# Latent layer: order of its first sums, place of the rotary work, transposes, and a last projection by token

## The chip, the cores and the metric

The kernel runs on one core of one Trainium2 chip. A core has five engines with queues of their own: TensorE (PE; PEld is its loading of weights), VectorE (DVE), ScalarE (ACT), GpSimd (POOL) and SyncE (SP), which issues most transfers. The metric is the device time of one execution in microseconds (us).

## The reference

Two blocks over 256 tokens of width 2048 in float32 stand one behind the other. The first has a mixer of chunked mLSTM heads and a gated convolution, and a feed-forward part; the second a layer of gated linear attention (GLA) and a latent layer (MLA). The change lies at the end of the GLA layer and in the latent layer, which computes:

```python
h = rms_norm(x, g_pre)                      # x = x + rms_norm(gla(...), g_post) before
c_q, c_kv, k_rope, gate = split(h @ w_in)   # 512, 512, 64, 2048
q = rms_norm(c_q, g_qa) @ w_qb              # 16 heads of 128 + 64 rotary
kv = rms_norm(c_kv, g_kva) @ w_kvb          # 16 heads of 128 (key) + 128 (value)
q_rope, k_rope = _rope(q_rope), _rope(k_rope)
s = einsum(q, k) * scale                    # causal
p = softmax(s); o = einsum(p, v)
y = (o * silu(gate)) @ w_out
x = x + rms_norm(y, g_post)
```

## The kernel before, in words

Activations lie feature by feature: `h` holds 16 blocks of 128 features (index k) by 256 tokens. All weights come as one stream, in the order in which `plan()` lists the products. SyncE loads it in pieces; each half of a piece (at most 1040 columns) is split into a high and a low half by ScalarE and VectorE (`need`, L313 and L314, tile `hl`). Inputs are split in the same way (`xhl`, `yg`, `cqkv`, `ohl`). A product of kind A takes the weights as the stationary operand and uses a 512-column and a 256-column matmul for each block k and 128 outputs (L360, L361). Kind S does the same with three 256-column ones (L383 to L385, as does kind C). Kind B takes the tokens as the stationary operand and has three matmuls per block k and half of the tokens (L373 to L375). Results lie in PSUM: two buffers `acc`, four small ones `sm`. Instructions go to the engines in the order of the program, apart from places that state a priority or a predecessor (`tc.issue_after`); each engine works through its queue in order.

The parts that the change touches:

- `out_norm` (L502) computes the GLA layer's output projection (`gwo`) and, at the end of the program, the latent layer's (`mwo`). It gathers squares, sums them over features by matmuls with one moving column (L529), takes the root (L533) and reciprocal (L534), and spreads the factor over a row by matmuls with a diagonal (L538). The result `Ry` stays in PSUM.
- `x3` (L1077) multiplies y by `Ry`, adds it to h (VectorE for blocks 0 and 1, GpSimd for pairs after that) and splits the sum into `xhl`, the input of the latent layer. `lazy` calls it up to four blocks ahead of the product that reads it. The first such product is `cq`, four blocks of 128 outputs: the first eight blocks k for all four, then the other eight for two outputs at a time.
- The heads come in four groups of four (L1195). Each group computes queries (`qn`), rotary queries (`qr`), keys (`kn`) and values (`mv`); `scaled` (L1193) moves results out of PSUM. `rope` (L1121) does the rotary part, partly on GpSimd.
- `attend` works through a head in three steps: scores and softmax; transposing the probabilities by a product with a diagonal of reciprocal sums (L1177 to L1179); the product with the values, the gate and the split. `pump` places these steps between the products of the next group; for the last group `drain` (L1225) issues them with no product between.
- At the end the last norm is applied, h added, and the output stored in eight parts (L1231 to L1233).

Of the kernel before, what the change touches and what calls it, by code (L numbers as in the profile page):

```python
# [45 lines left out]
def plan():  # L46
    g = []

    def add(name, kind, blocks, k0, nk):
# [11 lines left out]
        g.append(dict(name=name, kind=kind, blocks=blocks, k0=k0, nk=nk, n=nk * n, order=order))  # L61
# [36 lines left out]
    add("cq", "A", [(W, _blk(i * P)) for i in range(4)], 0, KD)  # L98
# [145 lines left out]
def build(tc, a, dump=None):  # L244
# [257 lines left out]
    def out_norm(name, IN, g, y):  # L502
# [569 lines left out]
    Ry = out_norm("gwo", YG, "g_post0", y)  # L1072
# [3 lines left out]

    def x3(k):  # L1077
# [197 lines left out]
```

## Time and profile before

| | |
|---|---|
| median of 3 runs | 2035.83 us (2035.56 to 2035.98) |
| profiled execution | 2035.79 us |
| its span, first to last instruction | 2034.1 us |
| TensorE busy (matmul) | 2003.1 us, 98% |
| VectorE, ScalarE, GpSimd busy | 1429.3, 1158.0, 390.0 us |
| mean granted TensorE clock | 0.992 of 2.4 GHz |
| read from memory | 381.52 MB, 189 GB/s over the span |

The span is counted from the first to the last instruction; the profiled execution's own time is 1.7 us longer. Matmuls overlap: the distance between two starts, not the duration of one, is what a matmul costs in a row of them. In a timeline the first number is the start, the second the duration, and a bracket tells how long the engine was idle before and what released it. A granted clock of 1.00 is 2.4 GHz, 0.50 is 1.2 GHz.

### The profile page before, as it was taken

How to read it: one execution, taken by the hardware profiler on the slowest of the kernel's cores; microseconds unless marked ns; L12 is line 12 of the kernel's file. 1: busy time of each engine (PE TensorE's matmuls, PEld its weight loads, DVE VectorE, ACT ScalarE, POOL GpSimd, SP SyncE). 2: the span in 40 equal slices, each digit the busy share in tenths (PEclk: the TensorE clock that was granted, in tenths of full speed). 3: DMA queues.
4: the chain of work that ended last, by engine and by line, in shares of the span. 5: the costliest groups of instructions: out<-in, count | busy, mean ns of one | idle time of the engine just before them, and what ended most of it. 6: DMA issues, size and time to landing. Idle time of an engine off the chain costs nothing. (4 is left out here: it accounts for less than half of the span.)

```text
span 2034.1 us, 30728 instructions
## 1 busy us (share of the span) xinstructions
PE 2003.1 (98%) x12460; PEld 1849.1 (91%) x12460; DVE 1429.3 (70%) x1764; ACT 1158.0 (57%) x1607; POOL 390.0 (19%) x330
## 2 busy tenths in 40 slices
PE   8999999999999999999999999999999999999997
PEld 8989999999999999999999999999999988989996
DVE  8778776666667888864588876676667568677754
ACT  6555555555556666644466666665566656644553
POOL 8411000001122111100011113411210124112312
PEclk9999999999999999999999999999999989999998
DMA  7544555555555555555555555545545545554243
GB/s 292 202 162 166 207 200 202 199 205 193 202 207 188 208 204 195 201 207 207 193 201 202 195 207 205 187 163 194 174 166 202 195 163 179 194 188 143 105 169 111
DMA packets 55839, 385.61 MB, mean 190 GB/s; under 512 B 6368, under 2 KB 7264, under 8 KB 10640
## 3 DMA queue, kind: packets, MB, share of 16 engines
q1 hardware_dynamic: 55440, 383.44, 52.2%
q8 instruction: 97, 1.59, 0.3%
q0 software_dynamic: 112, 0.20, 0.1%
q14 instruction: 46, 0.38, 0.1%
q10 hardware_dynamic: 144, 0.01, 0.0%
HBM read 381.52 MB, written 2.10 MB: 189 GB/s over the span
## 5 line engine op out<-in xcount | busy, mean ns | idle before, releaser
L314 DVE TENSOR_TENSOR hl<-raw,hl 128x1024 fp32r<-128x1024 f32 (+2 forms) x723 | 945.1, 1316 | 349.0 <-ACT hl L313 348.2
L360 PE MATMUL acc<-xhl,hl 128*128 128x512 f32 x3440 | 1140.8, 385 | 8.7 <-DVE xhl L436 6.0
L313 ACT ACTIVATE hl<-raw 128x1024 fp32r<-128x1024 f32 (+2 forms) x723 | 756.5, 1050 | 383.4 <-PE acc L361 249.9
L361 PE MATMUL acc<-xhl,hl 128*128 128x256 f32 x3440 | 940.8, 274 | 1.2 <-DVE hl L314 1.2
L360 PEld LDWEIGHTS acc<-xhl,hl 128*128 128x128 f32 x3440 | 653.1, 190 | 104.4 <-issue 5.4
L361 PEld LDWEIGHTS acc<-xhl,hl 128*128 128x128 f32 x3440 | 663.4, 193 | 2.9 <-DVE hl L314 2.5
L360 PE MATMUL acc<-ghl,hl 128*128 128x512 f32 x688 | 225.4, 382 | 0.0
L413 ACT ACTIVATE t<-acc 128x512 f32<-128x512 f32 x138 | 82.1, 595 | 191.9 <-PE acc L361 171.2
L361 PE MATMUL acc<-ghl,hl 128*128 128x256 f32 x688 | 187.5, 273 | 0.0
L414 DVE TENSOR_TENSOR u<-acc,t 128x512 f32<-128x512 f32 x138 | 94.9, 688 | 102.3 <-ACT t L413 102.3
L419 POOL TENSOR_TENSOR uR<-u,R 128x512 f32<-128x512 f32 x51 | 68.9, 1350 | 447.0 <-DVE u L414 439.6
L360 PEld LDWEIGHTS acc<-ghl,hl 128*128 128x128 f32 x688 | 130.0, 189 | 18.1
L361 PEld LDWEIGHTS acc<-ghl,hl 128*128 128x128 f32 x688 | 132.1, 192 | 0.0
L457 POOL TENSOR_TENSOR ss<-ss,sq 128x512 f32<-128x512 f32 x41 | 65.6, 1599 | 222.9 <-ACT sq L452 213.3
L373 PE MATMUL acc<-hl,xhl 128*128 128x344 f32 x288 | 89.7, 311 | 0.0
L375 PE MATMUL acc<-hl,xhl 128*128 128x344 f32 x288 | 89.3, 310 | 0.2 <-DVE hl L314 0.2
L374 PE MATMUL acc<-hl,xhl 128*128 128x344 f32 x288 | 89.0, 309 | 0.0
L828 POOL TENSOR_TENSOR m<-u 128x256 f32<-128x256 f32 x16 | 25.0, 1562 | 320.3 <-DVE u L826 306.2
L816 PE MATMUL acc<-hmxc,hl 128*128 128x512 f32 x256 | 84.7, 382 | 0.0
L360 PE MATMUL acc<-mg,hl 128*128 128x512 f32 x256 | 83.9, 382 | 0.0
L864 ACT ACTIVATE cv<-uR,vec 128x256 f32<-128x256 f32 x86 | 47.0, 593 | 57.9 <-POOL uR L419 57.9
L360 PE MATMUL acc<-ohl,hl 128*128 128x512 f32 x224 | 73.7, 383 | 0.0
(517 smaller groups left out, 2481.1 us busy)
## 6 DMA issues: line engine op xcount, KB each, us to landing
raw<-stream SPq DMA_DIRECT2D x330, 1024.0 KB, 4.8
raw<-stream SPq DMA_DIRECT2D x21, 1032.0 KB, 4.8
raw<-stream SPq DMA_DIRECT2D x4, 512.0 KB, 6.6
out<-y SPq DMA_DIRECT2D x8, 256.0 KB, 2.1
raw<-stream SPq DMA_DIRECT2D x1, 1028.0 KB, 4.9
h<-xT SPq DMA_DIRECT2D x2, 512.0 KB, 9.0
raw<-stream SPq DMA_DIRECT2D x1, 1008.0 KB, 4.8
raw<-stream SPq DMA_DIRECT2D x1, 988.0 KB, 4.9
```

What stands on the lines that cost most here:

```text
L313: S.activation(hl[:, 0, x:y_], src, AF.Copy)
L314: V.tensor_tensor(hl[:, 1, x:y_], src, hl[:, 0, x:y_].bitcast(F32), op=ALU.subtract)
L360: PE.matmul(o, lhsT=wh, rhs=both(x), start=(k == 0), stop=False)
L361: mm = PE.matmul(o[:, T:2 * T], lhsT=wl, rhs=part(x, 0), start=False, stop=(k == nk - 1))
L373: PE.matmul(o, lhsT=xh, rhs=both(wh), start=(k == 0), stop=False)
L374: PE.matmul(o, lhsT=xl, rhs=both(wh), start=False, stop=False)
L375: mm = PE.matmul(o, lhsT=xh, rhs=both(wl), start=False, stop=(k == nk - 1))
L413: S.activation(halves(t[:, :nb]), out_of(ps[:, :nb, T:2 * T]), AF.Copy)
L414: V.tensor_tensor(halves(u[:, :nb]), out_of(ps[:, :nb, 0:T]), halves(t[:, :nb]), op=ALU.add)
L419: (eng or V).tensor_tensor(w[:, :nb], u[:, :nb], bc2(R)[:, :nb], op=ALU.mult)
L457: (eng or G).tensor_tensor(self.ss, self.ss, sq, op=ALU.add)
L816: PE.matmul(o, lhsT=wh, rhs=both(x), start=(k == 0), stop=False)
```

## The change

There are five edits.

- Start of the latent layer. `x3` is written as sums (`x3_sum`) and splits (`x3_split`), chained on each engine by `queued`. Sums are issued four blocks ahead of the splits. `cq` has all four outputs together for twelve blocks k instead of eight (`joint`). `out_norm` gets matmuls whose results nobody reads (`spin`): four after the column sums, seven after the row. Six of the squares for the second norm move between the products that follow.
- Rotary work. `rope` is cut into `rope_parts` (the multiplications) and the addition. The multiplications stand behind the keys' products, the addition behind the values'. One half of the value scaling goes from VectorE to ScalarE.
- Transposes. ScalarE divides the probabilities by their sums in place; TensorE's `transpose` takes the place of the product with a diagonal, and GpSimd no longer builds one.
- Last projection. `mwo` becomes kind B: three groups of 512 outputs and two of 256, tokens in the partitions. Its first group hosts the last four heads: a callback `mid` issues one of their steps ahead of each block k from 2 to 11 and the rest at 12. h is transposed to tokens beside the products (`h_by_token`), and the post-norm gain comes as a broadcast load `gT` (1 MB in the buffer) on GpSimd's queue.
- End. The last group of 256 outputs runs all blocks for the first 128 tokens, then for the others. Norm and sum are one VectorE instruction per piece, with the token's factor as a scalar; five pieces for each half of the tokens are stored. The output array is (256, 2048).

```diff
+LAST = ((0, 512), (512, 512), (1024, 512), (1536, 256), (1792, 256))
...
-            order = [(k, b) for k in range(nk // 2) for b in range(nb)]
-            order += [(k, b) for q in range(2) for k in range(nk // 2, nk) for b in (2 * q, 2 * q + 1)]
+            order = [(k, b) for k in range(joint) for b in range(nb)]
+            order += [(k, b) for q in range(2) for k in range(joint, nk) for b in (2 * q, 2 * q + 1)]
...
-    add("cq", "A", [(W, _blk(i * P)) for i in range(4)], 0, KD)
+    add("cq", "A", [(W, _blk(i * P)) for i in range(4)], 0, KD, 12)
...
-    for js in TAIL:
-        add("mwo", "A" if len(js) == 2 else "S", [(W, _blk(j * P)) for j in js], 0, KD)
+    for c, n in LAST:
+        add("mwo", "B", [(W, _blk(c, n))], 0, KD, fresh=c + n == D)
...
+                if mid and k:
+                    st["mm"] = mm.ins
+                    mid(k)
...
+    def spin(n):
+
+        ps = sm()
+        for i in range(n):
+            PE.matmul(ps[:, 0:P], lhsT=ones, rhs=ident, start=True, stop=True)
...
+        spin(before)
...
+        spin(behind)
...
-    Ry = out_norm("gwo", YG, "g_post0", y)
+    Ry = out_norm("gwo", YG, "g_post0", y, 4, 7)
...
+    def queued(e, f):
+
+        if e in chain:
+            with tc.issue_after(chain[e]):
+                i = f()
+        else:
+            i = f()
+        chain[e] = i.ins
+
+    def x3_sum(k, n, eng=V):
+        yk, hk = y[:, k:k + n], h[:, k:k + n]
+        queued("V", lambda: V.tensor_tensor(yk, yk, Ry[:, None, :].to_broadcast([P, n, T]), op=ALU.mult))
+        queued("V" if eng is V else "G", lambda: eng.tensor_tensor(hk, hk, yk, op=ALU.add))
+
+    def x3_split(k):
+        g = vc("g_pre1", k)
+        v = X_(k).rearrange("p (a s i) -> p s a i", a=2, s=2)
+        src = halves(h[:, k])
+        queued("S", lambda: S.activation(v[:, 0], src, AF.Identity, scale=g))
+        queued("V", lambda: V.scalar_tensor_tensor(v[:, 1], src, g, v[:, 0].bitcast(F32), op0=ALU.mult,
+                                                   op1=ALU.subtract))
+
     def x3(k):
-        if k > 1 and k % 2:
+        if k % 2:
             return
-        n = 1 if k < 2 else 2
-        yk, hk = y[:, k:k + n], h[:, k:k + n]
-        V.tensor_tensor(yk, yk, bc2(Ry)[:, 0:n], op=ALU.mult)
-        (V if k < 2 else G).tensor_tensor(hk, hk, yk, op=ALU.add)
-        for i in range(n):
-            last = split(X_(k + i), h[:, k + i], vc("g_pre1", k + i))
         if k == 0:
-            with tc.issue_after(last[0]), tc.issue_after(last[1]):
+            x3_sum(0, 1)
+            x3_sum(2, 2, G)
+            x3_split(0)
+            x3_sum(1, 1)
+            x3_sum(4, 2, G)
+            x3_split(1)
+            with tc.issue_after(chain["V"]), tc.issue_after(chain["S"]):
                 need(st["sub"])
+            return
+        for i in range(2):
+            x3_split(k + i)
+        if k + 4 < KD:
+            x3_sum(k + 4, 2, G)
...
+    for q in range(2):
+        for k in range(6 * q, 6 * q + 6, 2):
+            st6.add(h[:, k:k + 2])
+        low_rank_in(1, sb, q, dense("ckv", X))
+    for k in (12, 14):
         st6.add(h[:, k:k + 2])
...
-        dg = tt("dg")
-        for qt in range(2):
-            G.tensor_scalar(dg[:, 0, qt * P:(qt + 1) * P], ident, rs[:, qt:qt + 1], None, op0=ALU.mult)
+        for qt, o, n in ((0, 0, P), (1, P, T)):
+            S.activation(p_[:, o:o + n], p_[:, o:o + n], AF.Copy, scale=rs[:, qt:qt + 1])
         yield
         pT = sm()
-        PE.matmul(pT[:, 0:P], lhsT=p_[:, 0:P], rhs=dg[:, 0, 0:P], start=True, stop=True)
-        PE.matmul(pT[:, P:T], lhsT=p_[:, P:T], rhs=dg[:, 0, P:T], start=True, stop=True)
-        PE.matmul(pT[:, T:T + P], lhsT=p_[:, T:T + P], rhs=dg[:, 0, P:T], start=True, stop=True)
+        for i_ in range(3):
+            PE.transpose(pT[:, i_ * P:(i_ + 1) * P], p_[:, i_ * P:(i_ + 1) * P], ident)
...
-        for p in range(2):
-            rope([(qr[:, p], 0, P)], u[:, p], (V, V, G, G))
+        parts = []
         for p in range(2):
             scaled(kn[:, 2 * p:2 * p + 2], dense("kn", XK), skv)
             pump(2)
+            parts.append(rope_parts(u[:, p], (V, V, G, G)))
         ps = dense("mv", XK)
-        for s in range(2):
-            V.tensor_scalar(vv[:, s], ps[:, s, :], skc[:, s:s + 1], None, op0=ALU.mult)
+        S.activation(vv[:, 0], ps[:, 0, :], AF.Copy, scale=skc[:, 0:1])
+        V.tensor_scalar(vv[:, 1], ps[:, 1, :], skc[:, 1:2], None, op0=ALU.mult)
+        for p in range(2):
+            rope([(qr[:, p], 0, P)], parts[p])
...
+    hT, yT = big(F32, (P, 2, D), name="hT"), big(F32, (P, 2, D), name="yT")
+    gT = big(name="gT")[:, 0:D]
+    nc.gpsimd.dma_start(gT, a["gpost"][0:1, :].to_broadcast([P, D]))
+    sums = stp.tile([P, 2, 4], F32, tag="sums", name="sums")
+    c_ = stp.tile([P, 2, 2], F32, tag="ct", name="ct")
+    warm = stp.tile([P, 1], F32, tag="warm", name="warm")
+
+    def h_by_token():
+        for k in range(0, KD, 4):
+            for t in range(2):
+                pt = sm()
+                for i in range(4):
+                    PE.transpose(pt[:, i * P:(i + 1) * P], h[:, k + i, t * P:(t + 1) * P], ident)
+                S.activation(hT[:, t, k * P:(k + 4) * P], pt, AF.Copy)
+            if k < 12:
+                yield
+
+    def evac_t(t, ps, at, n, total):
+        o = tt("sq").rearrange("p a t -> p (a t)")
+        S.activation(o[:, 0:n], ps, AF.Square, accum_out=total)
+        V.tensor_tensor(yT[:, t, at:at + n], ps, gT[:, at:at + n], op=ALU.mult)
+
+    for c, (at, n) in enumerate(LAST[:-1]):
+        if c == 0:
+            ps = dense("mwo", OX, lambda k: k > 1 and (pump() if k < 12 else drain()))
+            side.append(h_by_token())
+        else:
+            ps = dense("mwo", OX)
+        for t in range(2):
+            evac_t(t, ps[:, t, 0:n], at, n, sums[:, t, c:c + 1])
+        pump()
     drain()
-
-    y = big(F32, (P, KD, T), name="y")
-    Ry = out_norm("mwo", OX, "g_post1", y)
-    for i in range(8):
-        yk, hk = y[:, 2 * i:2 * i + 2], h[:, 2 * i:2 * i + 2]
-        V.tensor_tensor(yk, yk, bc2(Ry), op=ALU.mult)
-        (V if i in (2, 5, 7) else G).tensor_tensor(yk, yk, hk, op=ALU.add)
-        nc.sync.dma_start(a["out"][:, 2 * i:2 * i + 2], yk)
+    V.tensor_tensor(sums[:, :, 0:2], sums[:, :, 0:2], sums[:, :, 2:4], op=ALU.add)
+    V.tensor_tensor(sums[:, :, 0], sums[:, :, 0], sums[:, :, 1], op=ALU.add)
+    V.tensor_scalar(c_[:, 0], sums[:, :, 0], 1.0 / D, EPS, op0=ALU.mult, op1=ALU.add)
+    S.activation(warm, c_[:, 0, 0:1], AF.Sqrt)
+    e = next(it)
+    un = iter(e["units"])
+    at, n = LAST[-1]
+    ws = []
+    for t in range(2):
+        ps = sm()
+        o = ps[:, 0:n]
+        for k in range(KD):
+            if t == 0:
+                ws.append(wunit(next(un)))
+            wh, wl = ws[k]
+            x = OX(k)
+            xh, xl = (x[:, (2 * t + s_) * P:(2 * t + s_ + 1) * P] for s_ in range(2))
+            PE.matmul(o, lhsT=xh, rhs=both(wh), start=(k == 0), stop=False)
+            PE.matmul(o, lhsT=xl, rhs=both(wh), start=False, stop=False)
+            PE.matmul(o, lhsT=xh, rhs=both(wl), start=False, stop=(k == KD - 1))
+        evac_t(t, o, at, n, sums[:, t, 1:2])
+        r = c_[:, 1, t:t + 1]
+        S.activation(r, sums[:, t, 1:2], AF.Sqrt, bias=c_[:, 0, t:t + 1], scale=1.0 / D)
+        V.reciprocal(r, r)
+        for x, y_ in ((1536, 2048), (0, 512), (512, 1024), (1024, 1344), (1344, 1536)):
+            V.scalar_tensor_tensor(yT[:, t, x:y_], yT[:, t, x:y_], r, hT[:, t, x:y_], op0=ALU.mult, op1=ALU.add)
+            nc.sync.dma_start(a["out"][t * P:(t + 1) * P, x:y_], yT[:, t, x:y_])
```

TensorE between the last product of `gwo` and `cq`, before (`ss` and `sq` hold the squares, `dg` the diagonal, `con` the ones and the identity):

```order
L385 MATMUL acc<-yg,hl 128x256
L529 MATMUL sm<-con,ss 128x1 x2
L529 MATMUL sm<-con,sq 128x1 x4
L538 MATMUL sm<-dg,con 128x128 x2
L360 MATMUL acc<-xhl,hl 128x512
L361 MATMUL acc<-xhl,hl 128x256
```

and of the change:

```order
L392 MATMUL acc<-yg,hl 128x256
L542 MATMUL sm<-con,ss 128x1 x2
L542 MATMUL sm<-con,sq 128x1 x2
L513 MATMUL sm<-con 128x128 x2
L542 MATMUL sm<-con,sq 128x1 x2
L513 MATMUL sm<-con 128x128 x2
L552 MATMUL sm<-dg,con 128x128 x2
L513 MATMUL sm<-con 128x128 x7
L364 MATMUL acc<-xhl,hl 128x512
L365 MATMUL acc<-xhl,hl 128x256
```

The eleven spin matmuls are the rows of L513; two of the first four have come to stand ahead of the last column sums.

VectorE in the first group of heads, from the rotary queries (`qru`) to the second keys, before (`mq` holds the group's results, `rw` rotary products):

```order
L1193 TENSOR_TENSOR qru<-acc,sq 128x256 x2
L1124 TENSOR_TENSOR rw<-qru,COS 128x256
L1127 TENSOR_TENSOR rw<-qru,SIN 32x256 x2
L1124 TENSOR_TENSOR rw<-qru,COS 128x256
L1129 TENSOR_TENSOR mq<-rw 128x256
L1127 TENSOR_TENSOR rw<-qru,SIN 32x256 x2
L314 TENSOR_TENSOR hl<-raw,hl 128x1024
L1129 TENSOR_TENSOR mq<-rw 128x256
L1193 TENSOR_TENSOR mq<-acc,skv 128x256 x2
L314 TENSOR_TENSOR hl<-raw,hl 128x1024
L1193 TENSOR_TENSOR mq<-acc,skv 128x256 x2
```

and of the change:

```order
L1240 TENSOR_TENSOR qru<-acc,sq 128x256 x2
L1170 TENSOR_TENSOR rw<-qru,COS 128x256
L318 TENSOR_TENSOR hl<-raw,hl 128x1024
L1173 TENSOR_TENSOR rw<-qru,SIN 32x256 x2
L1240 TENSOR_TENSOR mq<-acc,skv 128x256 x2
L1170 TENSOR_TENSOR rw<-qru,COS 128x256
L318 TENSOR_TENSOR hl<-raw,hl 128x1024
L1173 TENSOR_TENSOR rw<-qru,SIN 32x256 x2
L1240 TENSOR_TENSOR mq<-acc,skv 128x256 x2
L1178 TENSOR_TENSOR mq<-rw 128x256
L318 TENSOR_TENSOR hl<-raw,hl 128x1024
L1178 TENSOR_TENSOR mq<-rw 128x256
```

The first pair of L1193 (L1240 in the change), the scaling of the first keys, stood behind both rotary halves and now stands behind one; both additions (L1129, now L1178) stand behind the second keys.

VectorE at the end of the program, before:

```order
L314 TENSOR_TENSOR hl<-raw,hl 128x1024
L519 TENSOR_SCALAR y<-acc,vec 128x256 x2
L534 RECIPROCAL oc<-oc 128x2
L537 TENSOR_SCALAR dg<-con,oc 128x128 x2
L1231 TENSOR_TENSOR y<-y,sm 128x512 x4
L1232 TENSOR_TENSOR y<-y,h 128x512
L1231 TENSOR_TENSOR y<-y,sm 128x512 x3
L1232 TENSOR_TENSOR y<-y,h 128x512
L1231 TENSOR_TENSOR y<-y,sm 128x512
L1232 TENSOR_TENSOR y<-y,h 128x512
```

and of the change:

```order
L1296 TENSOR_TENSOR yT<-sm,gT 128x256
L1331 RECIPROCAL ct<-ct 128x1
L1333 SCALAR_TENSOR_TENSOR yT<-yT,ct,hT 128x512 x3
L1333 SCALAR_TENSOR_TENSOR yT<-yT,ct,hT 128x320
L1333 SCALAR_TENSOR_TENSOR yT<-yT,ct,hT 128x192
L1296 TENSOR_TENSOR yT<-sm,gT 128x256
L1331 RECIPROCAL ct<-ct 128x1
L1333 SCALAR_TENSOR_TENSOR yT<-yT,ct,hT 128x512 x3
L1333 SCALAR_TENSOR_TENSOR yT<-yT,ct,hT 128x320
L1333 SCALAR_TENSOR_TENSOR yT<-yT,ct,hT 128x192
```

The products and sums over the whole output (L1231, L1232) were all behind the last matmul; now one half of the tokens (the first five rows) is done before the other half's product ends.

## Rows read from the trace of the kernel before

**Rows 1.** Waits of TensorE over the whole span: us in total, times, longest.

```profile
PE acc L360 <- DVE xhl L436: 6.0, 5, 2.6
PE acc L373 <- DVE mq L1193: 4.2, 4, 2.5
```

**Rows 2.** Stretches: length, busy time of each engine, granted clock, DMA share, GB/s.

```profile
1662.00:1668.00 6.00, 2.53 (x22) 2.28 (x20) 3.82 (x11) 2.44 (x6) 0.59 (x1) 0.90 0.00 0
1668.00:1676.00 8.00, 7.37 (x22) 5.95 (x23) 7.14 (x10) 4.63 (x8) 4.33 (x3) 0.50 0.36 131
1920.00:1930.00 10.00, 9.91 (x67) 9.07 (x65) 7.69 (x29) 5.95 (x19) 2.69 (x5) 1.00 0.30 110
```

**Rows 3.** Timeline of TensorE, start of the latent layer: start, us, [idle before].

```profile
1662.17 0.28 PE L385 MATMUL acc<-yg,hl 128*128 128x256 f32 x1
...
1667.87 0.77 PE L360 MATMUL acc<-xhl,hl 128*128 128x512 f32 x1 [2.60 <-DVE xhl L436]
...
1676.68 0.54 PE L360 MATMUL acc<-xhl,hl 128*128 128x512 f32 x1
...
1677.17 0.38 PE L360 MATMUL acc<-xhl,hl 128*128 128x512 f32 x1
...
1677.50 0.38 PE L360 MATMUL acc<-xhl,hl 128*128 128x512 f32 x1
```

**Rows 4.** Timeline of VectorE at the same place.

```profile
1665.31 0.75 DVE L1082 TENSOR_TENSOR y<-y,sm 128x256 f32<-128x256 f32 x2 [0.61 <-PE sm L538]
1665.98 0.75 DVE L1083 TENSOR_TENSOR h<-h,y 128x256 f32<-128x256 f32 x2
...
1667.25 0.48 DVE L436 SCALAR_TENSOR_TENSOR xhl<-h,vec,xhl 128x256 fp32r<-128x256 f32 x1
...
1668.24 1.69 DVE L314 TENSOR_TENSOR hl<-raw,hl 128x1024 fp32r<-128x1024 f32 x1
```

**Rows 5.** Timeline of TensorE, first group of heads, value product.

```profile
1826.31 0.45 PE L373 MATMUL acc<-hl,cqkv 128*128 128x512 f32 x1 [2.47 <-DVE mq L1193]
...
1828.14 0.63 PE L373 MATMUL acc<-hl,cqkv 128*128 128x512 f32 x1
1828.57 0.63 PE L374 MATMUL acc<-hl,cqkv 128*128 128x512 f32 x1
...
1830.66 0.38 PE L373 MATMUL acc<-hl,cqkv 128*128 128x512 f32 x1
1830.87 0.38 PE L374 MATMUL acc<-hl,cqkv 128*128 128x512 f32 x1
```

**Rows 6.** Timeline of VectorE ahead of that product.

```profile
1820.11 1.73 DVE L1127 TENSOR_TENSOR rw<-qru,SIN 32x256 f32<-32x256 f32 x2
```

**Rows 7.** Timeline of TensorE, one head's transposing products.

```profile
1912.39 0.39 PE L1177 MATMUL sm<-dg,p__17210 128*128 128x128 f32 x2
1912.61 0.39 PE L1178 MATMUL sm<-dg,p__17210 128*128 128x128 f32 x2
```

**Rows 8.** Transposes at line 931: min/median/max ns, first and last start.

```profile
L931 PE MATMUL sm<-con,gkc x2: 277/278/278, 1331.8 to 1333.1; 128*16 128x128 f32 x2
```

**Rows 9.** Timeline, end of the program.

```profile
2018.39 0.28 PE L385 MATMUL acc<-ohl,hl 128*128 128x256 f32 x1
2018.51 0.51 PE L529 MATMUL sm<-con,ss 128*128 128x1 f32 x4
2018.77 0.38 ACT L518 ACTIVATE sq<-acc 128x256 f32<-128x256 f32 x1 [5.03 <-PE acc L385]
...
2021.53 2.48 DVE L1231 TENSOR_TENSOR y<-y,sm 128x512 f32<-128x512 f32 x4 [0.61 <-PE sm L538]
...
2028.87 1.04 DVE L1232 TENSOR_TENSOR y<-y,h 128x512 f32<-128x512 f32 x1
```

**Rows 10.** DMA from 2015 us on: packets, MB, share; then KB, us to landing.

```profile
q1 hardware_dynamic: 1152, 2.10, 29.0%
...
out<-y SPq DMA_DIRECT2D x8, 256.0 KB, 2.1
```

More of the change, by code (lines that the diff above doesn't have):

```diff
@@ L47, in plan, with add @@
     g = []
-    def add(name, kind, blocks, k0, nk):
+    def add(name, kind, blocks, k0, nk, joint=8, fresh=False):
         n = sum(len(c) for _, c in blocks)
@@ L56, in add @@
         elif nb == 4:
-            order = [(k, b) for k in range(nk // 2) for b in range(nb)]
-            order += [(k, b) for q in range(2) for k in range(nk // 2, nk) for b in (2 * q, 2 * q + 1)]
+            order = [(k, b) for k in range(joint) for b in range(nb)]
+            order += [(k, b) for q in range(2) for k in range(joint, nk) for b in (2 * q, 2 * q + 1)]
         else:
             order = [(k, b) for k in range(nk) for b in range(nb)]
-        g.append(dict(name=name, kind=kind, blocks=blocks, k0=k0, nk=nk, n=nk * n, order=order))
+        g.append(dict(name=name, kind=kind, blocks=blocks, k0=k0, nk=nk, n=nk * n, order=order, fresh=fresh))
     W = "w_in"
@@ L121, in plan @@
         e["units"] = []
+        if e["fresh"] and cur:
+            subs.append(cur)
+            cur = 0
         for _ in range(e["n"] // n):
@@ L500, in second, with out_norm @@
         V.tensor_tensor(dst, w, c_, op=ALU.mult)
-    def out_norm(name, IN, g, y):
+    def spin(n):
+        ps = sm()
+        for i in range(n):
+            PE.matmul(ps[:, 0:P], lhsT=ones, rhs=ident, start=True, stop=True)
+    def out_norm(name, IN, g, y, before=0, behind=0):
         st_ = Stat("a")
@@ L1075, in build @@
     X_ = X
+    chain = {}
+    def queued(e, f):
[16 more added lines that the diff above has]
+                                                   op1=ALU.subtract))
     def x3(k):
-        if k > 1 and k % 2:
+        if k % 2:
             return
-        n = 1 if k < 2 else 2
-        yk, hk = y[:, k:k + n], h[:, k:k + n]
-        V.tensor_tensor(yk, yk, bc2(Ry)[:, 0:n], op=ALU.mult)
-        (V if k < 2 else G).tensor_tensor(hk, hk, yk, op=ALU.add)
-        for i in range(n):
-            last = split(X_(k + i), h[:, k + i], vc("g_pre1", k + i))
-        if k == 0:
-            with tc.issue_after(last[0]), tc.issue_after(last[1]):
-                need(st["sub"])
+        if k == 0:
+            x3_sum(0, 1)
[5 more added lines that the diff above has]
+            with tc.issue_after(chain["V"]), tc.issue_after(chain["S"]):
+                need(st["sub"])
+            return
[3 more added lines that the diff above has]
+            x3_sum(k + 4, 2, G)
     X = lazy(X_, x3, 4)
@@ L1115, in build, with rope_parts @@
         low_rank_in(0, sa, q, ps[q])
-    for k in range(0, KD, 2):
+    for q in range(2):
[3 more added lines that the diff above has]
+    for k in (12, 14):
         st6.add(h[:, k:k + 2])
-    for q in range(2):
-        low_rank_in(1, sb, q, dense("ckv", X))
-    def rope(dst, u, eng):
+    def rope_parts(u, eng):
         w = tt("rw")
@@ L1127, in rope @@
             eng[i].tensor_tensor(w[32 * o:32 * o + 32, 1], u[32 * i:32 * i + 32], SIN[32 * i:32 * i + 32], op=ALU.mult)
+        return w
+    def rope(dst, w):
         for d, lo, hi in dst:
@@ L1140, in build @@
             uR = times_R(ukr, R, 1)
[L1141 removed]
+            rope([(kr[0:64, 0], 0, 64), (kr[64:128, 1], 64, 128)], rope_parts(uR[:, 0], (V, V, G, G)))
         s = times_R(u, R, eng=G)
@@ L1255, in host_arrays @@
         "wgk2": np.ascontiguousarray(i["l0_gla_w_gk2_2"]),
+        "gpost": i["l1_post_norm_2"].reshape(1, D),
         "pos": np.ascontiguousarray(i["positions_2"].reshape(1, T)),
@@ L1268 @@
         a[n] = nc.dram_tensor(n, v.shape, mybir.dt.from_np(v.dtype), kind="ExternalInput").ap()
-    a["out"] = nc.dram_tensor("out", (P, KD, T), F32, kind="ExternalOutput").ap()
+    a["out"] = nc.dram_tensor("out", (T, D), F32, kind="ExternalOutput").ap()
     with tile.TileContext(nc) as tc:
@@ L1273 @@
     got = r.results[0]["out"]
-    return np.ascontiguousarray(got.transpose(2, 1, 0)).reshape(1, T, D)
+    return np.ascontiguousarray(got).reshape(1, T, D)
```

1 line of the change is left out of this document (removed).

## The prediction

> **What bounds the kernel now.** I read the busy shares first: TensorE is busy for 2003.1 of 2034.1 us, so only time in which it waits, runs at the lower clock or does avoidable work can be won. The list of its waits comes next [rows 1]. Two entries lie inside the changed code: 6.0 us in five waits for the halves of the latent layer's first input (xhl), and 4.2 us in four waits of the value product (L373) for VectorE's scaling of the keys (L1193). The stretches then show what a wait costs beyond itself [rows 2]: from 1662 to 1668 us TensorE has 2.5 us of work in 6, and from 1668 to 1676 its granted clock is 0.50, the 1.2 GHz level. The timelines give the places [rows 3 to 6]. The last view is the end [rows 9]: the last product of the last projection begins at 2018.39 and ends at 2018.67, the span ends at 2034.1, so 15.4 us follow in which TensorE has next to nothing to do. The sum is made against the profiled execution, 2035.8 us with a span of 2034.1; the median of the runs is the same to 0.1 us.
>
> **Start of the latent layer.** Before, the last product of the layer ahead begins at 1662.17 and the first of `cq` at 1667.87. The norm's chain in between stays. Behind its result VectorE's order changes from two products y, two sums h, a product over two blocks and the split to one product, one sum, one product over two blocks, the split. From 1665.31 this is 0.33 + 0.33 (pairs of 256 columns start 0.67 apart [rows 4]) + 0.62 (four of 512 columns in 2.48 [rows 9]) + 0.48 for the split [rows 4], so the first `cq` product can begin near 1667.2: 0.6 earlier.
>
> The eleven spin products (four around the column sums, seven behind the row) stand where TensorE waits anyway: an fp32 product of 128 columns is two instructions and starts 0.22 after the one ahead [rows 7], so seven take 1.55 and end near 1666.8, before 1667.2. Their own cost is put at 0; without that cover it would be at most 0.4. Their effect is the clock. From 1667.87 to 1676.68 there are 12 pairs (a 512-column and a 256-column product) that at the full clock start 0.33 apart [rows 3]; 12 x 0.33 = 3.96 of 8.81, and about 0.8 of the rest is one of the short waits, so the lower clock costs 4.0. I take it that TensorE, with seven full products in front of `cq` and at most some 0.5 us idle behind them, stays at 2.4 GHz: -4.0. The four short waits (6.0 - 2.6 = 3.4 [rows 1]) come from sums on GpSimd that are ready late; they are now issued four blocks ahead, and the joint order up to block 12 halves what `cq` asks for per time in blocks 8 to 11: -3.4. What is late next is VectorE itself. Per two blocks it has two splits (0.48 each), one product (0.62) and one weight split (about 1.2, 1.69 beside GpSimd [rows 4]), 2.8 to 3.3, while TensorE wants 8 pairs x 0.33 = 2.6. Over seven such steps that is 1.4 to 4.9; I take +1.9, near the lower end, because GpSimd works only part of the time. Sum: -0.6 - 4.0 - 3.4 + 1.9 = **-6.1**.
>
> **Rotary work behind the keys.** Before, both rotary halves (L1127, 1.73 for two narrow products [rows 6]) stand on VectorE ahead of the first keys' scaling, whose PSUM buffer the value product needs. Now the first scaling stands behind one half in the first group of heads and ahead of both in the other three. First group: the wait of 2.47 [rows 5] shrinks to an estimated 0.3, and the clock need not fall: 12 value products from 1826.31 to 1830.66 would take 12 x 0.215 = 2.6 and took 4.35, -1.7 more. Other groups: 4.2 - 2.5 = 1.7, all gone. Late next is the second keys' scaling, needed 5.2 us later by the next query product, which is enough for one rotary half and a weight split. Moving half of the value scaling to ScalarE costs nothing on the path: ScalarE is busy 6.0 of 10 us there [rows 2]. Sum: **-5.6**, bounds -5.9 and -2.
>
> **Transposes.** Each of 16 heads has three products of 128 columns against a diagonal, two instructions and 0.22 each [rows 7]. A transpose is one instruction, as line 931 shows [rows 8]. I take half, 0.11: the column sums, four instructions with one moving column and a full weight load each, fit in 0.51, the last one's own latency included [rows 9], so a weight load alone keeps them about 0.1 apart. 48 x 0.11 = -5.3. The 32 new transposes of h beside the last product cost 32 x 0.11 = +3.5. The normalization moves from GpSimd to two ScalarE instructions per head, hidden as long as the transposes come four steps later. Sum: **-1.8**, bounds -6.2 (0.055 each) and +7.1 (0.22 each).
>
> The Trainium skill (TensorE: Matmul & The Clock Gate, section Terms) calls the transpose mode four times faster for FP32; by that the term would be -6.2. The same page of the Trainium skill, Part 4: PE-mode transpose, gives about 275 ns for a transpose inside a kernel, which speaks against this change; as a price per transpose the term would be 48 x 0.055 + 32 x 0.275 = +11.4. The trace has just that duration, 277 ns [rows 8], but an ordinary product lasts as long by itself while its successors start far sooner [rows 9], so I read it as a latency.
>
> **Last product.** By columns streamed the token-major form costs the same: per 512 outputs and block six products of 512 columns (0.215 apart [rows 5]), 1.29, against four pairs at 0.33, 1.31. 256-column products start 0.11 apart [rows 9], so the two narrow groups cost the same as well. Inside the first group the last four heads find cover: before, they ran almost alone, but the wait that shows is only 0.1 in 10 us [rows 2]; I take **-0.5** (0 to -2). What is queued behind the new waits: VectorE's first product with gT waits for a 1 MB load on GpSimd's queue, and the weight splits stand behind it; the load is issued behind the last rotary products, a whole group ahead.
>
> **The end.** Token block 0 is finished while block 1's 48 products (5.3 us) run. After the last product: square 0.38 beginning 0.1 later [rows 9], about 0.2 to read its sum, the product with gT 0.45, a reciprocal 0.17, so the first piece starts 1.3 after. Five pieces of 2048 columns in all take 2.5 at the rate of four 512-column products in 2.48 [rows 9]. The stores are the limit: 2.10 MB took 29.0% of 19.1 us, 5.5, so 1.05 MB needs 2.8; a store lands 2.1 after its issue, 0.7 of it transfer [rows 10]. 1.3 + 0.6 + 1.4 + 2.8 = 6.1. Before, the last store landed near 2032.0 (2029.91 + 2.1) and the span ended 2.1 later; 6.1 + 2.1 = 8.2 against 15.4: **-7.2**. Bounds: with pieces at the 1.04 of the last sum [rows 9], -6.1; with stores fully hidden but the last, -7.9.
>
> Sum: -6.1 - 5.6 - 1.8 - 0.5 - 7.2 = -21.2; 2035.8 - 21.2 = **2014.6**.
>
> **Rivals.**
> The clock falls all the same before `cq`: spins alternate with waits, as column sums do now. Then 4.0 comes back, 2018.6. For it: the 1.2 GHz stretch follows a gap with some products in it [rows 2]. Chance 0.12.
> The transposes cost what the products did, or more: 0.22 each gives -1.8 to +7.1, 2023.5; at 0.275, 2027.7. Against it: one instruction in place of two. Chance 0.09.
> They cost 0.055: 2010.2. Chance 0.05.
> ScalarE delays the transposes: it waits in order for the reciprocal between exponential and normalization, with weight splits behind. Each of the four groups would lose about 1 us, 2018.6. Against it: ScalarE has 4 us in 10 free. Chance 0.08.
> Slower than before: gT lands late. VectorE, in order, stops at its first product with gT, no weights are split, and TensorE stops when the three pieces in stock are used, each worth two blocks of 1.29, so 7.7 us after the first group's end. Each us of lateness beyond that is a us lost; from 29 us past the group's end (21.2 + 7.7) the change loses, and at 33 it gives 2040. For it: a wide load from one row by a queue that before moves little. Against it: the load has a whole group of the last product in front (16 x 1.29 us, and four heads). Chance 0.02.
> The forecast's case has 0.64 and a range of its own of 2010.5 to 2018.5. The range that leaves out no more than 0.2 is 2009.5 to 2021. About 0.2% (4 us) is what a measurement of this kernel can tell from no change; every case but the last lies beyond it on the fast side, with some room for terms that fail together: faster 0.95, same 0.02, slower 0.03.
>
> **What would show it.** A granted clock of 1.0 from 1668 on and waits of `cq` under 2 us in sum show the first term; no wait over 0.5 us at the value product, the second; transposes starting 0.11 apart, the third; about 8 us from the last product to the end of the span, the last. Wrong would be a low clock in `cq`, transposes 0.2 or more apart, or TensorE waiting for weights inside the last projection.

## The result, and the profile after

The changed kernel takes 2017.76 us (median of 4 runs, 2017.47 to 2018.6) against 2035.69 us of the kernel before (4 runs, 2034.54 to 2035.98): a ratio of 0.9914, 95% interval 0.9896 to 0.9931, 17.9 us less. 2014.6 had been predicted, so 3.2 us are missing from a gain of 21.2. Both profiled executions lie close to these medians: 2035.79 and 2017.47 us, spans of 2034.1 and 2015.8.

The page of the kernel after, its busy times:

```profile
PE 1995.2 (99%) x12386; PEld 1839.8 (91%) x12386; DVE 1426.8 (71%) x1762; ACT 1167.3 (58%) x1641; POOL 356.8 (18%) x287
```

These averages hide where the time went. I cut both traces at six starts of matmuls that exist in both kernels, and compare lengths (us):

| stretch | before | after | difference | predicted |
|---|---|---|---|---|
| up to the last `gwo` product | 1662.17 | 1662.43 | +0.26 | 0 |
| from there to the first `cq` product | 5.70 | 5.67 | -0.03 | -0.6 |
| to the last product that reads `xhl` | 142.30 | 140.96 | -1.34 | -5.5 |
| to the end of the first value product | 22.86 | 19.32 | -3.54 | -3.9 |
| to the end of the fourth value product | 86.49 | 80.32 | -6.17 | -5.7 |
| to the last product of all | 98.87 | 99.33 | +0.46 | +1.7 |
| to the end of the span | 15.71 | 7.77 | -7.94 | -7.2 |

The last column distributes the prediction's own terms: -5.6 for the rotary work is 3.9 in the first group and 1.7 in the others, 12 heads' transposes (36 x 0.11) fall into the fifth row, the other 12 transposes, the 32 new ones and the hosting into the sixth. The last row rests on spans given to 0.1 us. One stretch is badly missed, the start of the latent layer.

TensorE's waits after, from 1662 us on (us in total, times, longest), which answer to [rows 1]:

```profile
PE acc L364 <- DVE xhl L1113: 5.2, 8, 1.0
PE acc L380 <- DVE mq L1240: 0.6, 1, 0.6
```

The value product's 4.2 us have become 0.6. The waits for `xhl` were 6.0 in five and are now 5.2 in eight, where the prediction's sign for its first term was under 2. The stretches of [rows 2] at the start of the latent layer, after (length, busy time of PE, PEld, DVE, ACT, POOL, granted clock, DMA share, GB/s):

```profile
1662.00:1668.00 6.00, 5.22 (x45) 4.83 (x43) 3.09 (x9) 1.38 (x4) 0.43 (x1) 1.00 0.00 0
1668.00:1676.00 8.00, 6.01 (x33) 5.08 (x34) 7.50 (x11) 5.39 (x9) 4.07 (x3) 1.00 0.30 94
1676.00:1690.00 14.00, 11.59 (x65) 9.65 (x65) 14.00 (x17) 7.23 (x14) 8.67 (x4) 1.00 0.34 107
```

The clock did what was forecast: 1.00 where it had been 0.50. But VectorE is busy for all 14 us of the last row and TensorE for 11.59. The timelines say why; TensorE's first product of a block after each wait, then VectorE and GpSimd over the same stretch (start, duration):

```profile
1679.06 0.48 PE L364 MATMUL acc<-xhl,hl 128*128 128x512 f32 x1 [0.45 <-DVE xhl L1113]
1682.60 0.48 PE L364 MATMUL acc<-xhl,hl 128*128 128x512 f32 x1 [0.66 <-DVE xhl L1113]
1686.14 0.48 PE L364 MATMUL acc<-xhl,hl 128*128 128x512 f32 x1 [0.66 <-DVE xhl L1113]
```

```profile
1675.78 0.68 DVE L1105 TENSOR_TENSOR y<-y,sm 128x512 f32<-128x512 f32 x1
1676.38 1.21 DVE L318 TENSOR_TENSOR hl<-raw,hl 128x1024 fp32r<-128x1024 f32 x1
1677.52 1.88 DVE L1113 SCALAR_TENSOR_TENSOR xhl<-h,vec,xhl 128x256 fp32r<-128x256 f32 x2
1679.32 0.67 DVE L1105 TENSOR_TENSOR y<-y,sm 128x512 f32<-128x512 f32 x1
```

```profile
1676.54 2.18 POOL L1106 TENSOR_TENSOR h<-h,y 128x512 f32<-128x512 f32 x1 [0.96 <-DVE y L1105]
1680.08 2.19 POOL L1106 TENSOR_TENSOR h<-h,y 128x512 f32<-128x512 f32 x1 [1.36 <-DVE y L1105]
```

Two blocks take 3.54 us, for which TensorE wants 2.6 (eight pairs of matmuls 0.33 us apart). The two splits (L1113) take 1.88 here and 0.87 where GpSimd rests (1672.58). GpSimd's sum is issued at 1676.54 beside the weight split (L318, until 1677.52) and ends at 1678.72; the splits begin at 1677.52 and end at 1679.40, 0.68 behind the sum's end. It looks like turns: the sum runs from the weight split's end for 1.2 us, and the splits, 0.87 long, take place behind it but for 0.2.

The trace of the kernel before held this price already, a pair of splits beside a sum on GpSimd and one without, then that sum:

```profile
1677.62 1.89 DVE L436 SCALAR_TENSOR_TENSOR xhl<-h,vec,xhl 128x256 fp32r<-128x256 f32 x2
1680.64 0.88 DVE L436 SCALAR_TENSOR_TENSOR xhl<-h,vec,xhl 128x256 fp32r<-128x256 f32 x2
```

```profile
1677.77 1.46 POOL L1083 TENSOR_TENSOR h<-h,y 128x512 f32<-128x512 f32 x1 [1.76 <-DVE y L1082]
```

The other places came out as foreseen. The value product of [rows 5], a head's transposes of [rows 7] and the end of [rows 9], after:

```profile
1823.34 0.45 PE L380 MATMUL acc<-hl,cqkv 128*128 128x512 f32 x1 [0.61 <-DVE mq L1240]
```

```profile
1908.91 0.49 PE L1226 MATMUL sm<-con,p__17303 128*128 128x128 f32 x3
```

```profile
2008.03 0.28 PE L1327 MATMUL sm<-hl,ohl 128*128 128x256 f32 x1
2008.34 0.38 ACT L1295 ACTIVATE sq<-sm 128x256 f32<-128x256 f32 x1 [4.56 <-PE sm L1327]
2008.62 0.19 ACT L1295 ACTIVATION_READ_ACCUMULATOR sq<-sm 128x1 f32 x1
2008.85 0.42 DVE L1296 TENSOR_TENSOR yT<-sm,gT 128x256 f32<-128x256 f32 x1 [1.96 <-ACT sq L1295]
...
2009.38 2.87 DVE L1333 SCALAR_TENSOR_TENSOR yT<-yT,ct,hT 128x512 f32<-128x512 f32 x5
2010.16 2.64 SPq L1334 DMA_DIRECT2D out<-yT  x5
```

Three transposes that last 273 ns each fit in 0.49, so they start 0.11 apart. VectorE finishes the last 128 tokens 4.2 us after the last product's start, and its stores run beside it. In that stretch the DMA engines are fully busy (the two last figures are the DMA share and GB/s):

```profile
2011.00:2013.50 2.50, 0.00 (x0) 0.00 (x0) 1.25 (x3) 0.00 (x0) 0.00 (x0) 0.70 1.00 371
```

### The profile page after: what moved, and what is told of

It reads as the page before. It is cut to its first block, busy times and chain, and to the rows that moved or that the text cites. A ratio compares the mean times of both kernels' runs of the same rounds, so it can differ in the third digit from the quotient of the medians.

```text
span 2015.8 us, 30530 instructions
## 1 busy us (share of the span) xinstructions
PE 1995.2 (99%) x12386; PEld 1839.8 (91%) x12386; DVE 1426.8 (71%) x1762; ACT 1167.3 (58%) x1641; POOL 356.8 (18%) x287
## 4 chain that ended last, share of the span: by engine, by line
PE 95%; DVE 3%; ACT 1%; issue 1%; DMA 0%; SPq 0%; DVEq 0%; POOL 0%; ACTq 0%
PE acc L364 48%; PE acc L365 24%; PE acc L380 4%; PE acc L382 4%; PE acc L381 4%; PE acc L831 3%; PE acc L832 1%; DVE hl L318 1%; PE acc L392 1%; PE acc L390 1%; PE acc L391 1%; DVE xhl L1113 1%; PE sm L1209 1%; PE sm L1210 1%; PE sm L1016 0%
## 5 line engine op out<-in xcount | busy, mean ns | idle before, releaser
L318 DVE TENSOR_TENSOR hl<-raw,hl 128x1024 fp32r<-128x1024 f32 (+2 forms) x723 | 949.0, 1321 | 341.1 <-ACT hl L317 340.0
L420 ACT ACTIVATE t<-acc 128x512 f32<-128x512 f32 x131 | 77.9, 595 | 183.0 <-PE acc L365 162.2
L421 DVE TENSOR_TENSOR u<-acc,t 128x512 f32<-128x512 f32 x131 | 90.2, 688 | 96.9 <-ACT t L420 96.7
L464 POOL TENSOR_TENSOR ss<-ss,sq 128x512 f32<-128x512 f32 x35 | 53.9, 1539 | 160.0 <-ACT sq L459 150.6
L364 PE MATMUL acc<-yg,hl 128*128 128x512 f32 x224 | 73.4, 382 | 0.0
```

Source lines behind the costliest of these rows:

```text
L318: V.tensor_tensor(hl[:, 1, x:y_], src, hl[:, 0, x:y_].bitcast(F32), op=ALU.subtract)
L364: PE.matmul(o, lhsT=wh, rhs=both(x), start=(k == 0), stop=False)
L420: S.activation(halves(t[:, :nb]), out_of(ps[:, :nb, T:2 * T]), AF.Copy)
L421: V.tensor_tensor(halves(u[:, :nb]), out_of(ps[:, :nb, 0:T]), halves(t[:, :nb]), op=ALU.add)
L464: (eng or G).tensor_tensor(self.ss, self.ss, sq, op=ALU.add)
```

## The experiments

In the changed kernel and its variants the lengths of the stretches repeat to 0.05 us wherever the code is the same (the last product's start to the end: 7.71 to 7.78), while the place of the last `gwo` product wanders between 1661.79 and 1664.55. In the two variants of the kernel before, the first products took 142.22 and 141.62 against 142.30 with the same code there; in the second the clock rose earlier (mean 0.79 over 1668 to 1676, before 0.50). So there 0.7 us is the limit, and more where the clock falls in one execution and not in another. So I judge by the stretches, and by the medians beside them. "Start" is the second row of the table above, "first products" the third.

| run | median us, ratio to before (95%) | start | first products |
|---|---|---|---|
| after | 2017.76, 0.9914 (0.9896 to 0.9931) | 5.67 | 140.96 |
| e1_no_spin | 2018.18, 0.9916 (0.9901 to 0.9931) | 5.22 | 140.94 |
| e2_spin_behind | 2016.76, 0.9910 (0.9896 to 0.9925) | 5.22 | 140.95 |
| e3_sums_on_vector | 2016.33, 0.9908 (0.9893 to 0.9922) | 6.32 | 138.40 |
| e4_short_sums | 2011.63, 0.9884 (0.9867 to 0.9900) | 5.67 | 135.69 |
| e9_short_no_spin | 2013.47, 0.9894 (0.9879 to 0.9909) | 5.22 | 137.02 |
| e8_mixed | 2015.44, 0.9902 (0.9889 to 0.9916) | 5.22 | 139.02 |

**What was the clock worth?** The filler products taken out, and the first four alone:

```diff
-    Ry = out_norm("gwo", YG, "g_post0", y, 4, 7)
+    Ry = out_norm("gwo", YG, "g_post0", y, 0, 0)      # e1_no_spin
+    Ry = out_norm("gwo", YG, "g_post0", y, 0, 7)      # e2_spin_behind
```

> The changed kernel without its eleven filler products ahead of and behind the first sum of squares. Both theories expect the granted clock to fall again at the start of the latent layer, near 0.50 for about 8 us. Theory A (the first query projection of the latent layer is paced by VectorE, whose block splits run beside GpSimd's sums and are slowed by them, so a faster TensorE only waits longer): about 0 us against the changed kernel, -0.5 to +1.5, since TensorE's waits there shrink by nearly what the clock costs. Theory B (the prediction's: the clock itself was worth 4.0 us, less some 0.4 for the filler that delays the norm chain): +3.6 us, 2021.4 us.

> The changed kernel with no filler product ahead of the sum of squares and still seven behind it. If the four filler products ahead of it only delay the norm chain: -0.4 us (2017.4 us) with the clock at 1.00 through the stretch. If they are what keeps the clock: the clock falls near 0.50 after the pause and the time is that of the kernel without any filler (by theory A about 0 us, by theory B +3.6 us).

Without filler the clock fell again; the stretch of `e1_no_spin`:

```profile
1668.00:1676.00 8.00, 6.23 (x20) 5.42 (x21) 7.47 (x13) 5.23 (x9) 3.25 (x3) 0.57 0.13 17
```

and the first products took 140.94 us against 140.96 at the full clock. The clock was worth nothing here: theory A, and B is out. The four products ahead cost 0.45 us (5.67 against 5.22), since they delay the column sums behind them (the root begins 1.77 us after the last `gwo` product's start, and 1.32 in `e2_spin_behind`); the seven behind keep the clock alone in `e2_spin_behind` (1.00 throughout).

**Is it VectorE's own work, or GpSimd beside it?** The sums moved to VectorE, and the sums on GpSimd cut short:

```diff
-            x3_sum(2, 2, G)   # also (4, 2, G) and (k + 4, 2, G)
+            x3_sum(2, 2)      # e3_sums_on_vector
```

```diff
     def x3_sum(k, n, eng=V):
         yk, hk = y[:, k:k + n], h[:, k:k + n]
+        if eng is not V:                               # e4_short_sums
+            hk, yk = hk[:, :, 0:32], yk[:, :, 0:32]
```

> The changed kernel with every input sum on VectorE and none on GpSimd. Theory A (the two engines slow each other: a pair of block splits took 1.89 us beside a GpSimd sum and 0.87 us alone): VectorE's load in two blocks becomes 0.87 + 0.67 + 1.21 less what contention adds, plus about 1.1 for the sum, some 3.2 to 3.5 us against 3.54 us now: -2 us, between -2.5 and 0. Rival C (VectorE's own work is the bound and GpSimd takes nothing from it): a sum of about 1.1 us is added to each of five periods of two blocks: +4 to +5 us.

> The changed kernel with GpSimd's input sums cut to the first 32 of 256 tokens of each block: most of the sum of the layer's input and the attention output is left out in blocks 2 to 15, all other work stays. Theory A (GpSimd's sums slow VectorE's splits): the split pairs go from 1.89 to near 0.9 us, VectorE's period falls to about 2.6 us, TensorE's waits in the first query projection all but vanish: -4 to -5 us, about 2013 us. Rival C (VectorE's own work is the bound): no change, within 0.5 us. Rival B would say the same as C here.

With more work on VectorE the first products became 2.56 us shorter (the start 0.65 longer, 1.91 less in sum), with less on GpSimd 5.27 shorter, a little more than expected. That settles it against C: GpSimd's sums cost VectorE more than the same sums cost on VectorE itself. VectorE in `e3_sums_on_vector`, one whole period of two blocks, 3.13 us:

```profile
1677.16 1.21 DVE L318 TENSOR_TENSOR hl<-raw,hl 128x1024 fp32r<-128x1024 f32 x1
1678.30 0.68 DVE L1106 TENSOR_TENSOR h<-h,y 128x512 f32<-128x512 f32 x1
1678.90 0.87 DVE L1113 SCALAR_TENSOR_TENSOR xhl<-h,vec,xhl 128x256 fp32r<-128x256 f32 x2
1679.69 0.68 DVE L1105 TENSOR_TENSOR y<-y,sm 128x512 f32<-128x512 f32 x1
1680.29 1.21 DVE L318 TENSOR_TENSOR hl<-raw,hl 128x1024 fp32r<-128x1024 f32 x1
```

and VectorE, then GpSimd, in `e4_short_sums`:

```profile
1676.41 1.21 DVE L318 TENSOR_TENSOR hl<-raw,hl 128x1024 fp32r<-128x1024 f32 x1
1677.54 0.94 DVE L1115 SCALAR_TENSOR_TENSOR xhl<-h,vec,xhl 128x256 fp32r<-128x256 f32 x2
...
1679.00 1.21 DVE L318 TENSOR_TENSOR hl<-raw,hl 128x1024 fp32r<-128x1024 f32 x1
```

```profile
1676.57 1.24 POOL L1108 TENSOR_TENSOR h<-h,y 128x64 f32<-128x64 f32 x1 [1.36 <-DVE y L1105]
```

A sum over 64 columns also takes 1.24 us when it is issued under a weight split, and ends at 1677.81, 0.27 after VectorE has gone on to the splits: nearly all of it is waiting. So each engine stops the other. VectorE's period is 2.59 us here (1676.41 to 1679.00). The period of the kernel after is the sum of turns: L1105 0.60, the weight split 1.14, about 1.0 in which GpSimd's sum alone goes on, the two splits 0.80, together 3.54. With the sum on VectorE the 1.0 becomes 0.60 (1678.30 to 1678.90): 3.13.

The Trainium skill (SBUF — State Buffer, section Who interferes with whom) has this as a rule: a VectorE instruction with two SBUF inputs and a GpSimd instruction that reads SBUF exclude each other for a whole instruction, whichever comes second waiting. The rows above agree: the sum waits for the weight split, the splits for the sum. I had not weighed it in the prediction.

**Does the clock matter where VectorE is not slowed?** `e4_short_sums` with the filler taken out, as in `e1_no_spin`:

> GpSimd's input sums cut to 32 of 256 tokens (most of the sum of the layer's input and the attention output is left out in blocks 2 to 15) and no filler products. Theory A (the clock was worth nothing only because VectorE set the pace): with the sums short VectorE keeps up with TensorE, so the fall of the clock now costs what TensorE loses in it, 2.5 to 4 us less the 0.45 us of filler: 2 to 3.5 us above the kernel with short sums and filler. If the clock does not matter there at all: the same as that kernel, or 0.45 us below it.

The first products took 1.33 us more (137.02 against 135.69), the start 0.45 less: +0.88 in sum, and +1.8 by the medians. The sign is theory A's, the size less than its 2 to 3.5. The stretches from 1667 to 1675 us in the kernel with filler and in the one without:

```profile
1667.00:1675.00 8.00, 6.72 (x38) 5.64 (x38) 7.50 (x15) 6.27 (x11) 2.66 (x4) 1.00 0.36 126
```

```profile
1667.00:1675.00 8.00, 7.63 (x31) 6.74 (x32) 7.50 (x14) 6.11 (x11) 2.70 (x4) 0.65 0.37 131
```

At the full clock TensorE still idles for 1.28 of these 8 us behind VectorE, 0.72 of it after the first product of `cq`, and the low clock fills that first. So even here the two limits overlap in part.

**A mix.** The first sum on GpSimd, the others on VectorE, seven fillers behind:

```diff
-    Ry = out_norm("gwo", YG, "g_post0", y, 4, 7)
+    Ry = out_norm("gwo", YG, "g_post0", y, 0, 7)
...
-            x3_sum(4, 2, G)   # also (k + 4, 2, G)
+            x3_sum(4, 2)
```

> The changed kernel with its first input sum on GpSimd, all others on VectorE, no filler products ahead of the sum of squares and seven behind it. If VectorE's whole load up to the last block sets the end of the first query projection: about the kernel with all sums on VectorE less 0.45 us for the filler, 2015.5 to 2016 us. If the later start that the two first sums gave (0.65 us) is lost for good when both are on VectorE: 1.1 us below that kernel, about 2015.2 us.

Start and first products together: 144.24 us, against 144.72 with all sums on VectorE and 146.63 after. The 1.10 us won at the start was given back but for 0.48, as the first expectation has it: VectorE's whole load up to its last split sets the end. The clock fell here too (0.84 over 1668 to 1676), but TensorE still waits about 0.2 us for the splits in each period from 1679 to 1689, at the full clock, so the lower clock is not what set it. This is the fastest complete kernel, 2.3 us below the kernel after by the medians and 2.39 by the stretches; the intervals of the two ratios overlap, so it is the stretch, from one profile each, that shows the gain.

**The rotary work and the transposes, each alone in the kernel before.**

```diff
-        for p in range(2):
-            rope([(qr[:, p], 0, P)], u[:, p], (V, V, G, G))
...
             scaled(kn[:, 2 * p:2 * p + 2], dense("kn", XK), skv)
             pump(2)
+            parts.append(rope_parts(u[:, p], (V, V, G, G)))      # e5_rotary_alone
...
+        for p in range(2):
+            rope([(qr[:, p], 0, P)], parts[p])
```

```diff
-        dg = tt("dg")
-        for qt in range(2):
-            G.tensor_scalar(dg[:, 0, qt * P:(qt + 1) * P], ident, rs[:, qt:qt + 1], None, op0=ALU.mult)
+        for qt, o, n in ((0, 0, P), (1, P, T)):
+            S.activation(p_[:, o:o + n], p_[:, o:o + n], AF.Copy, scale=rs[:, qt:qt + 1])   # e6_transposes_alone
...
-        PE.matmul(pT[:, 0:P], lhsT=p_[:, 0:P], rhs=dg[:, 0, 0:P], start=True, stop=True)
...
+        for i_ in range(3):
+            PE.transpose(pT[:, i_ * P:(i_ + 1) * P], p_[:, i_ * P:(i_ + 1) * P], ident)
```

> The kernel before with one part of the change: the rotary products are made ahead of the value projection, their sums behind it, and ScalarE scales one half of the values. If the waits at the value product come from VectorE's rotary work alone, as the prediction has it: -5.6 us against the kernel before, 2030.1 us (from -4.5 to -5.7, since 0.6 us of wait stayed at the first of the four products in the changed kernel). If the gain at those places came from the start of the latent layer, which runs just ahead of the first of them: -3 us or less.

> The kernel before with one part of the change: ScalarE normalises the attention weights by row and TensorE transposes them in one pass, in place of three products against a diagonal matrix that GpSimd scales. By the prediction's term (48 transposes that start 0.11 us apart in place of 48 products 0.22 us apart): -5.3 us against the kernel before, about 2030 us. If ScalarE's two extra passes hold the transposes up: 0 to -2.6. If the first two of three transposes gain less than the spacing says because TensorE waits for the normalised rows at each head: about -3.

| from the last `xhl` product | before | e5 | e6 | after |
|---|---|---|---|---|
| to the end of the first value product | 22.86 | 19.31 | 21.18 | 19.32 |
| to the end of the fourth | 86.49 | 84.07 | 80.32 | 80.32 |
| to the last product | 98.87 | 99.45 | 97.14 | 99.33 |
| median us, ratio to before (95%) | | 2030.58, 0.9977 (0.9968 to 0.9985) | 2027.07, 0.9960 (0.9947 to 0.9972) | |

The rotary move alone gives -3.55 - 2.42 + 0.58 = -5.4 in these stretches, -4.6 by the medians. Of the +0.58, 0.56 lies at the last heads' products with the diagonal, which take 4.61 us from start to next start against 4.05; their weight loads wait for GpSimd's diagonals (0.34 us at 1923.21).

The kernel with the transposes alone is shorter by 1.68, 6.17 and 1.73 in these rows, but the 1.68 is not the edit's: no attention has run by then, TensorE waits 2.47 us for the keys as before, and only the clock behind that wait differs. Before, then `e6_transposes_alone`:

```profile
1827.00:1830.50 3.50, 3.50 (x10) 2.74 (x10) 2.09 (x4) 0.00 (x0) 0.00 (x0) 0.53 0.71 276
```

```profile
1827.00:1830.50 3.50, 3.50 (x18) 3.04 (x18) 2.33 (x5) 1.06 (x1) 0.00 (x0) 1.00 0.77 281
```

That leaves -6.17 - 1.73 = -7.9 (-8.2 by the medians), still far more than the 5.3 expected, and in the second row all that the whole change gives. So the waits of the last three value products go by either edit. In the kernel before, GpSimd ahead of the second of these products, and VectorE:

```profile
1847.99 1.27 POOL L1174 TENSOR_SCALAR dg<-con,p__16627 128x128 f32<-128x128 f32 x2 [3.43 <-DVE p__16627 L1171]
1849.35 3.69 POOL L1127 TENSOR_TENSOR rw<-qru,SIN 32x256 f32<-32x256 f32 x4
```

```profile
1851.16 0.42 DVE L1129 TENSOR_TENSOR mq<-rw 128x256 f32<-128x256 f32 x1 [1.40 <-POOL rw L1127]
```

GpSimd's share of the rotary work stood behind the diagonals (`dg`), which waited 3.43 us for a reciprocal; VectorE then stood idle for 1.40 us for it, in front of the keys' scaling (4.2 us in the three later groups together). Without diagonals GpSimd starts the rotary share earlier, and `e6_transposes_alone` keeps one wait at a value product, at the first, where no attention has run yet:

```profile
PE acc L373 <- DVE mq L1191: 2.5, 1, 2.5
```

**Hosting the last heads.** They are finished ahead of the last projection instead:

```diff
-            ps = dense("mwo", OX, lambda k: k > 1 and (pump() if k < 12 else drain()))
+            drain()
+            ps = dense("mwo", OX)
```

> The changed kernel with the last heads' attention finished ahead of the last product instead of inside its first column group. By the prediction's term for this: slower by 0.5 us (between 0 and 1.5). If attention's short products beside a long column group cost nothing in either place: 0. If putting them inside costs TensorE time (weights in and out of turn): faster by up to 1.

2017.82 us, and 99.53 against 99.33 from the fourth value product to the last product: hosting is worth 0.2 us, within the prediction's bounds (0 to 2) and under its 0.5.

**The end's stores.**

```diff
-            nc.sync.dma_start(a["out"][t * P:(t + 1) * P, x:y_], yT[:, t, x:y_])
+        nc.sync.dma_start(a["out"][t * P:(t + 1) * P, :], yT[:, t, :])
```

> The changed kernel with one store of 1.05 MB per half of the tokens at the end, behind the five scalings, in place of five stores of 96 to 256 KB behind one scaling each. If the end rests on stores that run beside VectorE's scalings: slower by 2 to 2.5 us, since 1.05 MB at the 384 GB/s of the trace takes 2.7 us that now lie mostly beside 2.87 us of scaling. If the end is fixed cost per store and issue (five issues took 2.64 us): no change, or up to 1 us faster.

The end became 9.22 us in place of 7.77, 2019.52 us (ratio 0.9924, 0.9911 to 0.9938): the first alternative, though 1.45 rather than 2 to 2.5. The rows of the store here and of the last pieces in the kernel after (count, KB, median us from issue to landing) have the reason:

```profile
out<-yT SPq DMA_DIRECT2D x2, 1024.0 KB, 3.9
```

```profile
out<-yT SPq DMA_DIRECT2D x2, 96.0 KB, 2.2
```

The last store is issued 4.24 us after the last product's start here and 4.37 there, and lands 3.86 us later here and 2.23 there: 1.5 us. A piece of 256 KB lands in 2.3 in the kernel after, so 768 KB more cost 1.6; by that estimate the 256 KB themselves would be 0.5 of their 2.3 and the rest fixed.

## Why the prediction was right, and where it was not

The total missed by 3.2 us and not by more partly by luck: 4.7 are missing at the start of the latent layer, and 2.0 came unforeseen in the last two stretches.

- **Start of the latent layer** (-6.1, measured -1.37): the mis-sized step is the last term, "I take +1.9, near the lower end, because GpSimd works only part of the time". It priced VectorE's two blocks at 2.8 to 3.3 us; they take 3.54, above even the upper end, because a GpSimd sum shuts the splits out for about 1 us. With 3.54 this term is 7 x (3.54 - 2.64) = 6.3, and the prediction's own sum -1.7. The row L314 at 1.69 beside GpSimd [rows 4] went into the upper end, but the splits stood at 0.48 each in both ends, though a pair took 1.89 beside a sum in the same trace (1677.62 above). The two terms ahead, -4.0 - 3.4, were nearly right as a pair: where VectorE keeps up (`e4_short_sums`, period 2.59) the first products took 6.6 us less than before. Singly they were no prices: "the lower clock costs 4.0" was worth nothing with VectorE setting the pace (`e1_no_spin`), since full speed only turns slow products into waiting, and 1.33 with short sums (`e9_short_no_spin`). The 0.6 us earlier start came to 0.48 without the four products ahead (5.22), which then cost 0.45, the "at most 0.4" for lost cover.
- **Rotary work** (-5.6): right in sum, -5.4 alone by the stretches. Of the -3.55 in the first group 1.9 is the wait (2.47 to 0.60) and 1.7 the clock's fall behind it, as taken; but that part hangs on the execution, for in `e6_transposes_alone` the clock stayed at 1.00 behind the same wait. The reason given, VectorE's order, holds for the first group; in the other three the late link was GpSimd behind its diagonals, which the transposes remove as well.
- **Transposes** (-1.8): 0.11 apart, as taken from the column sums. The Trainium skill's 275 ns (TensorE: Matmul & The Clock Gate, Part 4: PE-mode transpose) is the duration in this trace, 273 ns, and not the price; nor does the distance show a quarter of the 0.22 us of the fp32 product, as the four times of its section Terms would have it, but half. In the kernel before they do more than the term says (-7.9 for -5.3), through GpSimd; together with the rotary work those waits count once.
- **Last product** (-0.5): 0.2 for the hosting. The sixth stretch came out 1.2 better than predicted. The starts in the two traces show where: the products with the diagonal took 4.05 us there, some waiting for GpSimd, and the transposes in their place 1.32, so -2.7 for the -1.3 taken; the 32 transposes of h took 3.2 instead of 3.5.
- **The end** (-7.2, measured -7.94): right, and by the reason given: the stores are the limit (DMA share 1.00 above), and the last one lands 6.3 us after the last product's end, at 2014.63, where 6.1 was taken. What is better than forecast is the tail behind that landing: 1.15 us and not 2.1. In the kernel before it was 1.28, as the last store landed at 2032.78 there and not near 2032.0. That the sum meets the bound for hidden stores, -7.9, is chance.

None of the rivals happened: the clock stayed up, the transposes cost what was taken, ScalarE delayed nothing (from 1800 us to the last product the only wait is the 0.6 us above), and `gT`, issued near 1909.4 and landed 7.6 us later, was first needed at 1942.7. What came was no rival but a term of the sum beyond its own upper end: VectorE as the bound of `cq` at full clock.

## What to carry to other kernels

Before a clock loss and the waits around it are added up, work out the period of every engine in that stretch at full clock; the longest one is what the stretch costs, and the other gains overlap with it. Take each instruction's time for that period from a row where it runs beside what it will run beside. An idle GpSimd is not free help for a VectorE that is the bound: look in the trace for the same instruction beside GpSimd and alone, and compare what VectorE loses (here 1.0 us per sum) with what the work would take on VectorE itself (0.60). And before a wait is put down to the order of the engine named, follow that engine's own wait one step further back.

## What the hardware showed that I had not expected

- VectorE and GpSimd took turns to the full: a pair of splits 0.87 us alone and 1.88 beside a sum, a sum over 64 columns 1.24 us when it is issued under a weight split, of which 0.27 lay behind VectorE's next start.
- Seven filler products behind the pause kept the granted clock at 1.00 in one kernel (`e2_spin_behind`); in another with the same seven (`e8_mixed`) it was 0.84 over 1668 to 1676. Behind one and the same wait of 2.47 us in front of the first value product it was 0.53 in the kernel before and 1.00 in `e6_transposes_alone`, in code that is the same. What makes the difference stays open.
- One store of 1024 KB landed in 3.9 us, one of 256 KB in 2.3.
